# Summing seven half products of a weight tile in PSUM instead of on VectorE

## The chip, the cores and the metric

The kernel runs on one core of one Trainium2 chip. The metric is device time in microseconds (us): the median of several executions, and beside it one execution that the hardware profiler recorded. In the profile PE is TensorE (PEld its weight loads), DVE is VectorE, ACT is ScalarE, POOL is GpSimd and SP is SyncE.

## The reference

One block of a hybrid backbone over 512 latent tokens with a prefix of 256 context tokens, model width 1024, all in float32. The change lies in the first of the two matrix products of each feed-forward layer:

```python
def swiglu(u, wi, wo):
    gate, up = jnp.split(u @ wi, 2, axis=-1)      # wi: 1024 x 5632
    return (jax.nn.silu(gate) * up) @ wo          # wo: 2816 x 1024

def ffn_half(t, m, s, nw, wi, wo):
    u = modulate(t, nw, m[3 * s], m[3 * s + 1])
    return t + 0.5 * m[3 * s + 2] * swiglu(u, wi, wo)

# in the block: first layer over 512 latent + 256 context tokens,
h = ffn_half(h, lat_m, 0, ...); hc = ffn_half(hc, ctx_m, 0, ...)
# then the token mixer (linear attention and a recurrence), then the second layer over the 512 latent tokens
h = ffn_half(h, lat_m, 2, ...)
return rmsnorm(h, final_norm_w)
```

## The kernel before

Features lie on the partitions, tokens on the free axis. Every operand of a matrix product is split into a high part and a low part (`split`, L70: a cast on ScalarE, L75, then a subtraction on VectorE, L76), and a product is the sum of three matmuls: high by high, high by low, low by high.

A tile of `wi` is 1024 input features by 256 output features. Both of its dimensions and the tokens are cut in halves, and the four quadrants (128 features by half of the tokens) are made from seven half products instead of eight, of sums and differences of the halves. `half_items` (L173) makes the seven weight operands, four of them by sums on GpSimd (L180, tile `ws`). The token operands are the halves of the modulated tokens `u`, and four sums `T[0]` to `T[3]` (`half_sums`, L203), named by `half_operands` (L197) in the order of use. `half_gemm` (L224) does one tile: seven times 12 matmuls (L237) of N columns, N = 384 in the first layer and 256 in the second. In the kernel before each half product has a PSUM bank of its own, seven of the eight per tile. ScalarE copies the first to SBUF (L240, tile `hu`), and VectorE makes all sums out of it and the other banks: seven additions in a tile (L229).

`half_pair` (L757) calls `half_gemm` twice, for a gate tile and for the up tile of the same features. `gate` puts SiLU on each finished quadrant (ScalarE, L763, in SBUF). `up` multiplies each quadrant into it (VectorE, L769), and `keep` (L744) splits a finished row of 128 features (`ah` on ScalarE, `al` on VectorE) for the second product. There are 10 such pairs in each layer, 20 tiles of `wi`, so 40 tiles and 280 half products in all. The first pair of each layer goes another way (`start_both`, `first_latent`, evacuated by L753 and L754).

Weights go through a ring of split pieces (six in the first layer, eight in the second): when a half product is done, `done_w` (L136) frees its piece, and the piece six or eight places on is split into it. Between the pairs stand the second products with `wo` (`down`, L779, matmuls in L167), and in the first layer the work of the modulation is spread between the half products by `fill` (VectorE L448 and L450, matmuls L473 and L510).

A scheduler orders the instructions of each engine when the kernel is built, by the order of the program and its own estimate of when operands are ready. On the chip each engine takes its list strictly in that order.

Of the kernel before, what the change touches and what calls it, by code (L numbers as in the profile page):

```python
# [17 lines left out]
P = 128  # L18
# [16 lines left out]
class Block:  # L35
    """The block with features on the partitions and tokens on the free axis."""
# [12 lines left out]
    # ---------------------------------------------------------------- helpers  # L49
# [4 lines left out]
    def psum(self, pairs):  # L54
        """PSUM as so many pairs of banks, and single banks."""
        self.banks.close()
        self.pairs = pairs
        pool = lambda n: self.banks.enter_context(self.tc.tile_pool(name=self.n("ps"), bufs=n, space=PSUM, reuse_waits="tile"))
        if pairs:
            self.ps = pool(pairs)  # L60
        self.pss = pool(8 - 2 * pairs)

    def big(self):
        """[128, 1024] in PSUM."""
        return self.ps.tile([P, 1024], F32, tag="mm", name=self.n("mm"))
# [12 lines left out]
    def load_raw(self, parts, kts):  # L78
        """parts: (dram matrix, first row, first column, columns)."""
# [13 lines left out]
    def ring(self):  # L93
        """Room for 512 columns of a split operand: hi, lo."""
# [4 lines left out]
    def load_w(self, parts, kts=KT):  # L99
        """Split weights as a list of pieces of two row tiles: hi, lo."""  # L100
# [9 lines left out]
    def stream(self, items):  # L110
        """Operands in the order of their use: (pieces of the ring, function that makes them)."""
# [5 lines left out]
    def grow(self, pool, slots, raws):  # L117
        """More room for the ring, used after the one that it has."""
# [21 lines left out]
    def piece_items(self, part):  # L140
        """A tile of weights as items of one piece each."""
# [15 lines left out]
    def gemm(self, jobs, segs, kts=KT, order=None):  # L157
        """jobs: (psum or list of banks, weights, first column, columns); segs: (first psum column, columns, x(kt) -> hi, lo)."""
# [13 lines left out]
    # ------------------------------------------------- products of halves  # L172
    def half_items(self, w, r0, c0):  # L173
        """Operands of the seven products of a [1024, 256] tile of weights cut in halves both ways, in their order."""
# [8 lines left out]
        def make(i):  # L183
            if i == 0:
                st["raw"] = self.load_raw([(w, r0, c0, 256)], KT)
                s3 = sub(a(0, 0), a(0, 1))
                s1 = sub(a(0, 1), a(1, 1), ALU.add)
                s2 = sub(s1, a(0, 0))
                st["w"] = [a(0, 0), a(1, 0), s3, sub(a(1, 0), s2), s2, a(1, 1), s1]
# [7 lines left out]
    def half_operands(self, u):  # L197
        """Token operands of the seven products: u(k, t, kt) -> hi, lo of half k of the features and half t of the tokens."""
        o = lambda k, t: lambda kt: u(k, t, kt)
        v = lambda j: lambda kt: self.T[j][kt]  # L200
        self.hx = [o(0, 0), o(1, 0), v(2), o(1, 1), v(1), v(3), v(0)]

    def half_sums(self, kt, x0, x1, last=None):  # L203
        """Sums of the halves of row tiles kt and kt + 4: x0 whole values of the first tokens, x1 of the others with the bias still to add;
        returns the first and the last sum, still whole."""
# [18 lines left out]
    def half_gemm(self, N, out, fill):  # L224
        """The products of one tile of weights: out(i, j) is where quadrant i, j (features, tokens) goes, out(i, j, c) follows it."""
        nc = self.nc
        banks = []
        t = self.tmp.tile([P, N], F32, tag="hu", name=self.n("hu"), bufs=2)
        add = lambda o, x, y: nc.vector.tensor_tensor(out=o, in0=x, in1=y, op=ALU.add)  # L229
        for i in range(7):  # L230
            h, l = self.next_w()
            ps = self.small()[:, :N]
            banks.append(ps)
            for kt in range(4):
                xh, xl = self.hx[i](kt)
                for j in range(3):
                    nc.tensor.matmul(ps, (h, h, l)[j][:, kt, :], (xh, xl, xh)[j], start=kt == 0 and j == 0, stop=kt == 3 and j == 2)  # L237
            self.done_w()
            if i == 0:
                nc.scalar.copy(t, ps)  # L240
            elif i == 1:
                c = out(0, 0)
                add(c, t, ps)
                out(0, 0, c)
            elif i == 4:
                add(t, t, ps)
                c22, c12 = out(1, 1), out(0, 1)
                add(c22, t, banks[2])
                add(c12, t, banks[3])
            elif i == 5:  # L250
                c = out(1, 0)
                add(c, c22, ps)
                out(1, 0, c)
            elif i == 6:
                add(c12, c12, ps)
                out(0, 1, c12)
                add(c22, c22, ps)
                out(1, 1, c22)
            fill(i)

    def useg(self, s, t0=0, w=None):
        """Segment of the modulated tokens of stream s (0 latents, 1 context) for gemm."""
# [15 lines left out]
    # ---------------------------------------------------------------- setup  # L278
    def columns(self, g, parts):
        """Vectors of the inputs as columns over the partitions, 128 features each."""  # L280
# [47 lines left out]
    def setup_rest(self):  # L328
        """The vectors that the first feed-forward layer doesn't need."""
# [22 lines left out]
    def lru_scales(self):  # L352
        """-8 softplus(-lam) per channel, with exp by exact halving steps and a short series."""
# [39 lines left out]
    # ---------------------------------------------------------------- adaLN  # L393
    def ada_first(self, c, t, whole):
        """256 features of chunk c for both streams on TensorE, as rows: of the whole map or of its parts; returns what is left to trace."""
# [22 lines left out]
    def ada_turn(self, c, t, rows):  # L418
        """The rows as columns."""
# [21 lines left out]
    def ada_mul(self, raw, acc, ns, k):  # L441
        """Products and sums over two row tiles on VectorE."""
# [18 lines left out]
    def ada_gate(self):  # L461
        """Gate of the first sub-layer on TensorE, in pieces to trace between other work."""
# [27 lines left out]
    def gate_cols(self, t, rows):  # L490
        """The rows as columns."""
# [10 lines left out]
    def ada_sum(self, acc, ns, dst, r0):  # L502
        """Sums over the partitions on TensorE, exact in two parts, and the rows to dst."""
# [1167 lines left out]
```

## Time and profile before

| what | us |
|---|---|
| median of three runs | 1595.04 |
| lowest and highest of the three | 1594.09, 1595.93 |
| span of the profiled execution, first to last instruction | 1593.6 |
| PE busy in it | 1543.3 |
| DVE busy | 1258.2 |
| ACT busy | 782.0 |
| POOL busy | 332.6 |

The profiled execution has no time of its own beside its span, which lies 0.5 to 2.3 us under the three runs. A matmul counts as busy until its modelled end, and matmuls overlap, so PE can be busy throughout and still have started its matmuls late: the distance from one start to the next tells how fast it goes.

### The profile page before, as it was taken

What the parts mean: (1) busy time and instruction counts of PE and PEld (TensorE: products, weight loads), DVE (VectorE), ACT (ScalarE), POOL (GpSimd) and SP (SyncE); (2) the same over time, 40 slices, a digit from 0 to 9 for tenths busy, and PEclk for the clock granted to TensorE, in tenths of its full rate; (3) what the DMA queues carried; (4) which work ended last, traced back from release to release, by engine and by line L of the source; (5) the groups of instructions that cost most, each with busy time, mean ns of one, the idle gap of its engine ahead of it and who ended that gap; (6) DMA issues with size and microseconds to landing.
All of it is one profiled execution on the core that took longest, in us unless ns stands there. A gap on an engine that the chain in (4) does not pass through costs nothing.

```text
span 1593.6 us, 24995 instructions
## 1 busy us (share of the span) xinstructions
PE 1543.3 (97%) x9288; PEld 1383.8 (87%) x9288; DVE 1258.2 (79%) x2232; ACT 782.0 (49%) x1353; POOL 332.6 (21%) x265
## 2 busy tenths in 40 slices
PE   7979999999999999999999999999998899999998
PEld 4778898999998987899897888878898898999897
DVE  5997899999997688776577577777768996797694
ACT  6354233432342457455354487777444644354355
POOL 0441121311322124000000100000016451451322
PEclk9999999999999999999999999999999999999999
DMA  9214434341533233121216223224443224233233
GB/s 335 78 47 146 123 96 139 91 146 57 159 113 95 82 106 107 33 64 47 68 62 186 73 64 90 78 68 140 153 149 115 67 80 143 70 107 120 93 113 113
DMA packets 169238, 167.83 MB, mean 105 GB/s; under 512 B 7683, under 2 KB 166685, under 8 KB 169117
## 3 DMA queue, kind: packets, MB, share of 16 engines
q1 hardware_dynamic: 168092, 163.88, 33.8%
q0 software_dynamic: 1024, 2.36, 0.5%
q8 instruction: 73, 1.20, 0.3%
q14 instruction: 49, 0.39, 0.1%
HBM read 164.08 MB, written 2.10 MB: 104 GB/s over the span
## 4 chain that ended last, share of the span: by engine, by line
PE 71%; DVE 12%; ACT 5%; issue 3%; POOL 1%; DVEq 0%; ACTq 0%
PE sm L237 27%; PE sm L167 22%; PE mm L167 16%; DVE wl L76 3%; PE mm L1255 1%; PE sm L1055 1%; DVE th L1288 1%; PE mm L1082 1%; PE sm L1002 1%; ACT wh L75 1%; DVE rg L1286 1%; ACT e L1274 1%; ACT th L1273 1%; DVE xc L1238 1%; ACT rg L1275 1%
## 5 line engine op out<-in xcount | busy, mean ns | idle before, releaser
L76 DVE TENSOR_TENSOR wl<-raw,wh 128x512 fp32r<-128x512 f32 x420 | 312.6, 755 | 96.4 <-ACT wh L75 93.9
L75 ACT CAST wh<-raw 128x512 fp32r<-128x512 f32 x420 | 254.7, 618 | 255.5 <-PE sm L167 107.0
L167 PE MATMUL sm<-ah,wh 128*128 128x512 f32 (+1 forms) x576 | 172.5, 341 | 0.0
L167 PE MATMUL sm<-al,wh 128*128 128x512 f32 (+1 forms) x576 | 172.5, 340 | 0.0
L167 PE MATMUL sm<-ah,wl 128*128 128x512 f32 (+1 forms) x576 | 172.2, 339 | 0.0
L75 ACT CAST wh<-ws 128x512 fp32r<-128x512 f32 x160 | 97.5, 618 | 127.3 <-PE sm L167 66.4
L167 PE MATMUL mm<-ul_lo,wh 128*128 128x512 f32 x352 | 141.6, 402 | 0.0
L167 PE MATMUL mm<-ul_hi,wh 128*128 128x512 f32 x352 | 140.9, 400 | 0.0
L167 PE MATMUL mm<-ul_hi,wl 128*128 128x512 f32 x352 | 139.8, 397 | 0.0
L76 DVE TENSOR_TENSOR wl<-ws,wh 128x512 fp32r<-128x512 f32 x160 | 128.5, 814 | 12.4 <-ACT wh L75 12.0
L450 DVE SCALAR_TENSOR_TENSOR acc<-apiece,cs,acc 128x256 f32<-128x256 f32 x224 | 121.3, 564 | 15.1 <-DMA apiece<-in_w_ada_dram 12.8
L180 POOL TENSOR_TENSOR ws<-raw 128x512 f32<-128x512 f32 x40 | 60.1, 1503 | 331.7 <-DMA raw<-in_ffn_wi_dram 155.8
L237 PE MATMUL sm<-u_hi,wh 128*128 128x384 f32 x320 | 108.8, 340 | 6.1 <-ACT s L753 6.1
L167 PEld LDWEIGHTS sm<-al,wh 128*128 128x128 f32 x576 | 98.4, 189 | 12.9 <-issue 0.2
L167 PEld LDWEIGHTS sm<-ah,wh 128*128 128x128 f32 x576 | 98.5, 188 | 12.8 <-ACT ah L75 0.3
L167 PEld LDWEIGHTS sm<-ah,wl 128*128 128x128 f32 x576 | 98.4, 188 | 12.6
L237 PE MATMUL sm<-u_hi,wl 128*128 128x384 f32 x320 | 108.4, 339 | 0.0
L237 PE MATMUL sm<-u_lo,wh 128*128 128x384 f32 x320 | 108.4, 339 | 0.0
L797 DVE SCALAR_TENSOR_TENSOR h_l<-sm,hg,h_l 128x512 f32<-128x512 f32 (+1 forms) x80 | 55.1, 693 | 46.5 <-PE sm L167 46.5
L1220 POOL DMA_DIRECT2D gwr<-in_lru_wr_dram x8 | 5.8, 730 | 376.2 <-PE mm L167 255.7
L606 POOL TENSOR_TENSOR ssq<-ssq,t 128x256 f32<-128x256 f32 (+1 forms) x30 | 28.0, 934 | 263.7 <-ACT t L604 263.5
L167 PEld LDWEIGHTS mm<-ul_hi,wh 128*128 128x128 f32 x352 | 66.2, 188 | 15.8 <-issue 0.5
(496 smaller groups left out, 4346.4 us busy)
## 6 DMA issues: line engine op xcount, KB each, us to landing
raw<-in_ffn_wi_dram SPq DMA_DIRECT2D x88, 512.0 KB
apiece<-in_w_ada_dram SPq DMA_DIRECT2D x112, 256.0 KB
raw<-in_ffn_wo_dram SPq DMA_DIRECT2D x48, 512.0 KB
raw<-in_w_in_dram SPq DMA_DIRECT2D x48, 512.0 KB
araw<-in_w_ada_dram SPq DMA_DIRECT2D x8, 1024.0 KB
raw<-in_w_o_dram SPq DMA_DIRECT2D x16, 512.0 KB
raw<-in_w_in_dram SPq DMA_DIRECT2D x16, 256.0 KB
raw<-in_w_out_gla_dram SPq DMA_DIRECT2D x8, 512.0 KB
```

Source lines behind the costliest of these rows:

```text
L75: nc.scalar.copy(hi, src)
L76: (nc.gpsimd if eng == "p" else nc.vector).tensor_tensor(out=lo, in0=src, in1=hi.bitcast(F32), op=ALU.subtract)
L167: nc.tensor.matmul(dst[:cols, d0 : d0 + width], wk, xs, start=(kt == 0 and i == 0), stop=(kt == kts - 1 and i == 2),)
L180: nc.gpsimd.tensor_tensor(out=t, in0=x, in1=y, op=op)
L237: nc.tensor.matmul(ps, (h, h, l)[j][:, kt, :], (xh, xl, xh)[j], start=kt == 0 and j == 0, stop=kt == 3 and j == 2)
L450: nc.vector.scalar_tensor_tensor(out=acc[:, s, :], in0=raw[:, kt, :], scalar=c, in1=acc[:, s, :], op0=ALU.mult, op1=ALU.add)
L606: (nc.vector if kt == KT - 1 or s else nc.gpsimd).tensor_tensor(out=acc, in0=acc, in1=dst, op=ALU.add)
L797: nc.vector.scalar_tensor_tensor(out=h, in0=o[s][:, t0 : t0 + w], scalar=self.hg[:, s, m : m + 1], in1=h, op0=ALU.mult, op1=ALU.add)
L1002: nc.tensor.matmul(ps[:, :DV], (xh, xl, xh)[i][:, kt, t0 : t0 + P], w[kt // 2][i // 2][:, kt % 2, :], start=kt == 0 and i == 0, stop=kt == ...
L1055: nc.tensor.matmul(ps[:, :DV], kt_[d][:, n, :], v[:, p, :], start=True, stop=True)
L1082: nc.tensor.matmul(dst, states[d][p][:, es], dec[d][0][:, t], start=False, stop=d == 1)
L1238: nc.vector.scalar_tensor_tensor(out=dst, in0=x[:, :, a0 + o : L - a1 + o], scalar=w(j), in1=dst, op0=ALU.mult, op1=ALU.add)
```

## The change

The seven half products of a tile are taken in another order and accumulate in four banks, in the order a, c, a, b, a, d, a. TensorE thus adds four of the seven into bank a. Quadrant (1,0) is what bank a holds after the seventh. The three earlier contents of bank a (after the first, third and fifth product) are copied by ScalarE to SBUF, in place of one copy before. VectorE adds these copies to the other banks: one addition for quadrants (0,0) and (1,1), two for (0,1), none for (1,0), whose SiLU or multiplication reads PSUM directly. The order of the token operands, of the weight operands and of three sums on GpSimd changes with it. `keep` now follows quadrants (0,1) and (1,0). The text of the diff also drops comments, left out here.

```diff
 def half_items ... make(i):
-                s3 = sub(a(0, 0), a(0, 1))
                 s1 = sub(a(0, 1), a(1, 1), ALU.add)
                 s2 = sub(s1, a(0, 0))
-                st["w"] = [a(0, 0), a(1, 0), s3, sub(a(1, 0), s2), s2, a(1, 1), s1]
+                s3 = sub(a(0, 0), a(0, 1))
+                st["w"] = [a(0, 0), a(1, 0), s2, s1, s3, sub(a(1, 0), s2), a(1, 1)]
...
 def half_operands(self, u):
-        self.hx = [o(0, 0), o(1, 0), v(2), o(1, 1), v(1), v(3), v(0)]
+        self.hx = [o(0, 0), o(1, 0), v(1), v(0), v(2), o(1, 1), v(3)]
...
 def half_gemm(self, N, out, fill):
-        banks = []
-        t = self.tmp.tile([P, N], F32, tag="hu", name=self.n("hu"), bufs=2)
-        add = lambda o, x, y: nc.vector.tensor_tensor(out=o, in0=x, in1=y, op=ALU.add)
-        for i in range(7):
+        copies = []
+
+        def copy(ps):
+            t = self.tmp.tile([P, N], F32, tag="hu", name=self.n("hu"), bufs=5)
+            nc.scalar.copy(t, ps)
+            copies.append(t)
+
+        bank = {}
+        for i, b in enumerate("acabada"):
             h, l = self.next_w()
-            ps = self.small()[:, :N]
-            banks.append(ps)
+            first = b not in bank
+            if first:
+                bank[b] = self.small()[:, :N]
+            ps = bank[b]
             for kt in range(4):
                 xh, xl = self.hx[i](kt)
                 for j in range(3):
-                    nc.tensor.matmul(ps, (h, h, l)[j][:, kt, :], (xh, xl, xh)[j], start=kt == 0 and j == 0, stop=kt == 3 and j == 2)
+                    nc.tensor.matmul(ps, (h, h, l)[j][:, kt, :], (xh, xl, xh)[j], start=first and kt == 0 and j == 0,
+                                     stop=kt == 3 and j == 2, skip_group_check=not first)
+            if i in (0, 2, 4):
+                copy(ps)
             self.done_w()
-            if i == 0:
-                nc.scalar.copy(t, ps)
-            elif i == 1:
-                c = out(0, 0)
-                add(c, t, ps)
-                out(0, 0, c)
+            if i == 1:
+                out(0, 0, copies[0], ps)
             elif i == 4:
-                add(t, t, ps)
-                c22, c12 = out(1, 1), out(0, 1)
-                add(c22, t, banks[2])
-                add(c12, t, banks[3])
+                out(1, 1, copies[2], bank["b"])
             elif i == 5:
-                c = out(1, 0)
-                add(c, c22, ps)
-                out(1, 0, c)
+                out(0, 1, copies[1], ps, bank["b"])
             elif i == 6:
-                add(c12, c12, ps)
-                out(0, 1, c12)
-                add(c22, c22, ps)
-                out(1, 1, c22)
+                out(1, 0, ps)
             fill(i)
...
 def half_pair(m):
-            def gate(i, j, c=None):
-                if c is not None:
-                    self.last_silu = nc.scalar.activation(c, c, AF.Silu)
-                return at(i, j)
-
-            def up(i, j, c=None):
-                if c is None:
-                    return self.tmp.tile([P, N], F32, tag="c", name=self.n("c"), bufs=3)
-                nc.vector.tensor_tensor(out=at(i, j), in0=at(i, j), in1=c, op=ALU.mult)
-                if j == 1:
+            add = lambda o, x, y: nc.vector.tensor_tensor(out=o, in0=x, in1=y, op=ALU.add)
+
+            def gate(i, j, x, y=None, z=None):
+                o = at(i, j)
+                if y is not None:
+                    add(o, x, y)
+                    if z is not None:
+                        add(o, o, z)
+                    x = o
+                self.last_silu = nc.scalar.activation(o, x, AF.Silu)
+
+            def up(i, j, x, y=None, z=None):
+                for t in (y, z):
+                    if t is not None:
+                        add(x, x, t)
+                nc.vector.tensor_tensor(out=at(i, j), in0=at(i, j), in1=x, op=ALU.mult)
+                if (i, j) in ((0, 1), (1, 0)):
                     keep(ss[i])
```

## Rows read from the trace of the kernel before

**Rows 1.** The page: busy time by engine, and slices of the span.

```profile
PE 1543.3 (97%) x9288; PEld 1383.8 (87%) x9288; DVE 1258.2 (79%) x2232; ACT 782.0 (49%) x1353; POOL 332.6 (21%) x265
...
DVE  5997899999997688776577577777768996797694
```

**Rows 2.** Waits of PE, whole span: total us, times, longest us.

```profile
PE sm L237 <- ACT s L753: 6.1, 2, 4.4
PE sm L237 <- DVE hu L229: 4.1, 4, 2.0
...
PE sm L473 <- DVE al L76: 2.1, 1, 2.1
PE sm L473 <- ACT ah L75: 1.8, 1, 1.8
```

**Rows 3.** Busy us by stage: PE, PEld, DVE, ACT, POOL, granted clock, DMA share, GB/s.

```profile
281.00:341.00 60.00, 60.00 (x352) 59.48 (x349) 58.32 (x105) 25.73 (x47) 14.54 (x10) 1.00 0.37 111
...
1246.00:1319.00 73.00, 66.17 (x516) 64.66 (x515) 72.04 (x108) 35.26 (x75) 37.18 (x27) 0.95 0.29 86
...
1269.20:1272.50 3.30, 3.30 (x18) 3.30 (x17) 3.30 (x8) 1.39 (x4) 0.94 (x1) 0.50 0.54 165
1372.00:1453.00 81.00, 81.00 (x678) 80.81 (x677) 77.58 (x133) 42.84 (x85) 36.53 (x23) 1.00 0.34 105
```

**Rows 4.** Timeline of DVE, two additions merged in a row, each layer.

```profile
296.81 1.00 DVE L229 TENSOR_TENSOR c<-hu,sm 128x384 f32<-128x384 f32 x2
...
1269.49 0.74 DVE L229 TENSOR_TENSOR s<-hu,sm 128x256 f32<-128x256 f32 x2
```

**Rows 5.** Groups of ACT by line: the copy of each layer (busy, mean ns).

```profile
L240 ACT COPY hu<-sm 128x384 f32<-128x384 f32 x17 | 8.0, 471 | 0.0
...
L240 ACT COPY hu<-sm 128x256 f32<-128x256 f32 x13 | 4.8, 367 | 0.0
```

**Rows 6.** Timeline of PE: starts of half products two and three of a tile.

```profile
297.87 0.34 PE L237 MATMUL sm<-u_hi,wh 128*128 128x384 f32 x1
...
299.95 0.34 PE L237 MATMUL sm<-T20h,wh 128*128 128x384 f32 x1
```

**Rows 7.** Timeline of ACT beside the tile of Rows 6.

```profile
302.35 0.83 ACT L75 CAST ah<-s 128x768 fp32r<-128x768 f32 x1 [5.91 <-DVE s L769]
303.09 0.62 ACT L75 CAST wh<-ws 128x512 fp32r<-128x512 f32 x1
```

**Rows 8.** Timeline of DVE up to that cast.

```profile
295.74 0.54 DVE L229 TENSOR_TENSOR hu<-hu,sm 128x384 f32<-128x384 f32 x1
...
298.81 0.54 DVE L769 TENSOR_TENSOR s<-s,c 128x384 f32<-128x384 f32 x1
299.27 1.51 DVE L450 SCALAR_TENSOR_TENSOR acc<-apiece,cs,acc 128x256 f32<-128x256 f32 x1
300.70 0.54 DVE L229 TENSOR_TENSOR c<-c,sm 128x384 f32<-128x384 f32 x1
...
301.77 0.55 DVE L769 TENSOR_TENSOR s<-s,c 128x384 f32<-128x384 f32 x1
```

**Rows 9.** Timeline of PE and of ACT in the first tile of all.

```profile
96.24 0.52 PE L237 MATMUL sm<-T20h,wh 128*128 128x384 f32 x1
...
99.09 0.62 ACT L75 CAST wh<-ws 128x512 fp32r<-128x512 f32 x1
```

**Rows 10.** Timeline of PE and ACT, start of the second layer.

```profile
1281.34 0.28 PE L237 MATMUL sm<-T10h,wh 128*128 128x256 f32 x1
1281.46 0.28 PE L237 MATMUL sm<-T10l,wh 128*128 128x256 f32 x1
...
1309.54 0.28 PE L237 MATMUL sm<-T20h,wh 128*128 128x256 f32 x1
...
1286.65 0.62 ACT L75 CAST wh<-ws 128x512 fp32r<-128x512 f32 x1
...
1316.15 0.60 ACT L75 CAST wh<-raw 128x512 fp32r<-128x512 f32 x1
```

## The prediction

> **What bounds the kernel now.** I read the page first: PE is busy 97% of the span, DVE 79%, but DVE's slices stand at 7 to 9 tenths in the feed-forward layers, at both ends of the span [rows 1]. Then busy time by stage. In the first layer, from 281 to 341 us, PE is busy all 60 us and DVE 58.3 of them; in the second, from 1372 to 1453, PE all 81 and DVE 77.6; only where the second layer begins, from 1246 to 1319, does PE fall behind (66.2 of 73) with DVE full (72.0) [rows 3]. Last the waits of PE. Matmul L237 waits 6.1 us for the evacuation before the first tile (L753), 4.1 us in four waits for an addition that still reads a bank (L229), and the filler's matmuls L473 wait 3.9 us for ACT and DVE [rows 2]. All of them lie at the beginnings of the two layers. So in the steady tiles PE sets the time, and DVE, nearly as busy, is late without PE noticing: bank and weights are ready long before PE needs them. Less work for DVE pays nothing there by itself. The question is whether PE stays free of DVE's lateness.
>
> **What is removed.** Three additions of seven per tile. A pair of them takes 1.00 us in the first layer and 0.74 in the second [rows 4], so one about 0.5 and 0.37, and a tile is relieved of 1.5 and 1.1 us of DVE: 20 x 1.5 + 20 x 1.1 = 52 us. By stage: four tiles in the 60 us leave DVE 52.3 there, eight tiles in the 81 leave 68.8, six in the 73 leave 65.4 [rows 3]. Three banks per tile come free; what that can give is the four waits for L229, 4.1 us [rows 2].
>
> **What is added on ACT.** Two copies per tile, 0.47 and 0.37 us [rows 5], 34 us in all. ACT is busy 25.7 of the 60 us and 42.8 of the 81 [rows 3]; with 3.8 and 5.9 more it stays near half. As work they cost nothing, as long as ACT isn't waiting when they come.
>
> **What stays.** The number of matmuls. Adding into a bank that holds a sum is what the later matmuls of each product do now, so I take no other rate. The sums on GpSimd are the same four in another order, their results used earlier or later by a product or two, with six or eight pieces of lead: nothing, and a few us for one late piece at most. No transfer is moved.
>
> **The new wait.** Half products three, five and seven write the bank that ACT has to have copied after one, three and five. One other product stands between: 2.08 us in the first layer [rows 6], 12 x 0.12 = 1.44 in the second [rows 10]. A copy and handing over, for which I add 0.1 us (an estimate: ACT starts 0.03 us after the multiplication that it waited for has ended [rows 7, 8], and there are two such steps), need 0.57 and 0.47. So the copy is hidden if ACT reaches it within about 1.3 or 0.8 us of the product's end, since that end lies 0.2 us behind the next start. ACT takes its list in order; when a cast (`ah`) or SiLU ahead of the copy waits for DVE, the copy waits too, and behind it now PE.
>
> Where ACT would be can be read from the old trace: the cast `wh` of the piece that a half product frees is ready at the same moment as the new copy, which stands directly ahead of it. In most of the 120 places this cast starts at once. Where not, the third product's start would be late by the cast's start, plus copy and handing over, less the old start:
> first tile of all: 99.09 + 0.57 - 96.24 = 3.4 us [rows 9];
> a steady tile of the first layer: 303.09 + 0.57 - 299.95 = 3.7, where ACT had waited 5.9 us for DVE's last multiplication [rows 6, 7];
> start of the second layer: 1286.65 + 0.47 - 1281.34 = 5.8, and the largest of all, 1316.15 + 0.47 - 1309.54 = 7.1 [rows 10].
> The lateness of one stretch of tiles between two down projections is one and the same queue: PE pays its largest value once. Read so, the ten stretches have 4.7, 0, 3.9, 3.7, 1.1, 2.7, 0 in the first layer and 7.1, 4.6, 1.3 in the second, 29 us together. This is the price if DVE's relief didn't reach the copies; with full relief it is nothing.
>
> **The relief, place by place.**
> *Start of the first layer.* The copy is 3.4 us late, but a tile later PE waits 3.9 us for the filler's split anyway [rows 2], so the new wait takes the place of the old one. I take -0.5. Ends: the wait stays beside the new one, +3.4; no copy late and the old wait gone, -3.9.
> *Steady tiles of the first layer.* In the tile of rows 7 the copy waits for the multiplication of quadrant (0,1), at 301.77. It now belongs to half product six instead of seven, with two additions and one weight split fewer ahead of it, 2 x 0.5 + 0.6; if it also passes the filler's L450 (1.51), 3.1 [rows 8]. I take 2.0, near the sure part: 1.7 of the 3.7 stays, 0.7 of the 2.7 in the same way. At the 3.9, two tiles before it give 3.0 more, and nothing stays; nor of the 1.1. Together +2.4, between 0 and 11.4.
> *Start of the second layer.* Two tiles lie before the 5.8: 5.8 - 2 x 1.1 = 3.6. Before the 7.1 lie five: 1.6, less than already paid. Of the waits for banks, 2.0 us lie ahead of that place and are in its times, and the other 2.1 behind it fall away: +1.5. Ends: -4.1 and +7.1.
> *Later tiles of the second layer.* The lateness grows by some 1.9 us per pair up to 4.6, and a pair is relieved of 2.2: nothing, at most 5.9.
> A long wait of PE costs more than itself: behind the one of 2.0 us the granted clock is 0.50, the lower level, from 1269.2 to 1272.5 [rows 3], and 3.3 us at half speed lose 1.65. One such stretch may come in the steady tiles and one may go at a start; I count none and keep 1.65 each way.
>
> Sum: -0.5 + 2.4 + 1.5 + 0 = +3.4 us. The profiled execution spans 1593.6, which gives 1597.0; the median of the runs lies 1.4 above that span, so 1598.4.
>
> **The rivals.**
> *The copies hold PE (slower).* The scheduler's list was made from its own estimate, and ACT stands behind DVE where that is too short; a list made for fewer additions can be as far off. Then the 29 us of lateness are paid less what falls away at the starts, 4.1 and 3.9: up to +21, with half of the relief +12, so 1607 to 1616. For it: ACT waits of 5.9 us [rows 7]. Against it: DVE has 8 us in 60 to spare after the change. It decides where ACT comes to a copy over 1.3 us after its product. The Trainium skill (PSUM — Partial Sum Buffer, Summary: rules for kernel authors) speaks for this rival: whoever reads PSUM while a matmul runs should target a different bank, and guard by bank. The traces so far show no half product that waits for such a reader inside its tile, since each had its own bank.
> *The starts gain (faster).* From 1246 to 1319 DVE is full; 6.6 us less work could pass to PE directly, and the waits for banks (4.1) and for the filler (3.9) would go with up to two stretches at half clock (3.3). All of it is -11; with half, some -6: 1589. It needs the copies on time at the starts, where DVE is most behind, so the relief would have to cover 3.4 and 5.8 us that I see covered by 1.5 to 2.2. The Trainium skill (Perfetto Trace Analysis, Optimization Strategy) speaks for it: the same gap again and again on the engine that should be full can mean too little PSUM. Here there are four such gaps, 4.1 us in 1594.
> *Nothing measurable.* DVE isn't on the path for most of the span, and the small terms cancel: 1593 to 1598. It is the lower part of my forecast.
>
> **Chances and range.** The forecast, +3.4 with its own range of -1 to +9 us, has 0.55; the copies 0.23; the starts 0.22. About 0.2% (3.2 us) is what a measurement of this kernel can tell from no change. The forecast lies on that line: 0.35 of it I give to no change, 0.20 to slower. So faster 0.22, same 0.35, slower 0.43. For 8 in 10 the range reaches into both rivals: 1588 to 1612.
>
> **What would show it.** Right: DVE's busy time falls to about 1206 us and ACT's rises to about 816; waits of L237 for L229 are gone; in their place stand waits of L237 for the new copy, the longest in the first pair after a down projection and at the start of the second layer, a handful, under 10 us together; most copies start within 0.2 us of their product. Wrong: waits for the copy in most tiles and the clock at half in steady stretches (the slower rival); no such waits over 1 us and both starts shorter (the faster one); another distance than 0.17 or 0.12 us between matmuls that add to a full bank.

## The result and the profile after

The changed kernel takes 1634.97 us (median of 4 runs, 1634.0 to 1637.5) against 1595.25 for the kernel before, run beside it (4 runs): a ratio of 1.0251, interval 1.0238 to 1.0264. It is 39.7 us slower, outside the range of 1588 to 1612. The profiled execution spans 1632.2 us, 38.6 more than that of before: over the span PE is idle 30.2 us longer and busy 8.4 us longer.

In the kernel after, the half products' matmul stands on L245, the copy on L232, the additions on L760, the SiLU on L769, the multiplication on L775. The page first, the lines that answer to [rows 1]:

```profile
PE 1551.7 (95%) x9288; PEld 1390.4 (85%) x9288; DVE 1237.2 (76%) x2112; ACT 812.9 (50%) x1433; POOL 338.6 (21%) x265
...
DVE  5996998978976688676577587769668984795684
```

DVE has 120 instructions fewer, as meant, but is only 21.0 us less busy (1258.2 to 1237.2), not 52. Then PE's waits, which answer to [rows 2]:

```profile
PE sm L245 <- ACT hu L232: 37.0, 20, 5.7
...
PE sm L245 <- ACT s L752: 6.2, 2, 4.4
```

The waits for an addition that still reads a bank (4.1 us) are gone; in their place PE waits 37.0 us in 20 places for the new copy, in 19 of them before the third half product of a tile. Busy time by stage, in stretches that hold about as many matmuls as those of [rows 3], and two short stretches behind a wait (columns as there):

```profile
285.00:349.00 64.00, 60.47 (x350) 59.20 (x348) 55.77 (x96) 30.24 (x57) 12.52 (x10) 1.00 0.35 108
1265.00:1343.00 78.00, 66.32 (x514) 65.29 (x514) 72.27 (x102) 42.47 (x92) 39.89 (x27) 0.93 0.27 86
1396.00:1487.00 91.00, 84.20 (x681) 82.88 (x680) 81.10 (x115) 49.97 (x105) 38.89 (x24) 0.98 0.34 103
...
1458.50:1461.90 3.40, 3.40 (x18) 3.40 (x18) 3.40 (x3) 1.13 (x4) 3.32 (x3) 0.50 0.40 131
...
1301.40:1304.70 3.30, 3.30 (x18) 3.30 (x17) 3.30 (x5) 1.71 (x4) 2.92 (x2) 0.51 0.50 153
```

The eight tiles in which PE was busy all of 81 us now take 91, and PE is idle for 6.8 of them. It is also busy 3.2 us longer with about as many matmuls. A part of that is clock: behind one of the waits below (1457.27) the granted clock is at 0.50, the lower level, for 3.4 us, which at half speed lose 1.7; the stage stood at 1.00 before. Where the rest of the 3.2 goes wasn't followed. The loss is in the steady tiles, not only where a layer begins.

A smaller part lies between the two layers, where PE now waits for DVE once (this wait isn't in the trace of before; why it comes wasn't followed):

```profile
PE sm L1008 <- DVE x L1134: 2.5, 1, 2.5
```

These are the third half products of six tiles of the second layer, PE's timeline (start, duration, in brackets the wait and what ended it):

```profile
1411.51 0.39 PE L245 MATMUL sm<-T10h,wh 128*128 128x256 f32 x1 [1.89 <-ACT hu L232]
...
1422.24 0.38 PE L245 MATMUL sm<-T10h,wh 128*128 128x256 f32 x1 [0.49 <-ACT hu L232]
...
1433.92 0.39 PE L245 MATMUL sm<-T10h,wh 128*128 128x256 f32 x1 [1.47 <-ACT hu L232]
...
1445.31 0.39 PE L245 MATMUL sm<-T10h,wh 128*128 128x256 f32 x1 [1.18 <-ACT hu L232]
...
1457.27 0.39 PE L245 MATMUL sm<-T10h,wh 128*128 128x256 f32 x1 [1.77 <-ACT hu L232]
...
1545.00 0.39 PE L245 MATMUL sm<-T10h,wh 128*128 128x256 f32 x1 [1.89 <-ACT hu L232]
```

Five tiles in a row pay, each anew. Why, is seen by following the last of these waits backwards through three engines. ACT:

```profile
1543.54 1.14 ACT L75 CAST ah<-s 128x512 fp32r<-128x512 f32 x2 [2.76 <-DVE s L775]
1544.58 0.36 ACT L232 COPY hu<-sm 128x256 f32<-128x256 f32 x1
1544.84 0.62 ACT L75 CAST wh<-raw 128x512 fp32r<-128x512 f32 x1
```

DVE:

```profile
1535.72 5.19 DVE L76 TENSOR_TENSOR wl<-ws,wh 128x512 fp32r<-128x512 f32 x3
1540.83 0.74 DVE L760 TENSOR_TENSOR hu<-hu,sm 128x256 f32<-128x256 f32 x2
1541.49 0.41 DVE L775 TENSOR_TENSOR s<-s,hu 128x256 f32<-128x256 f32 x1
1541.82 0.68 DVE L76 TENSOR_TENSOR wl<-raw,wh 128x512 fp32r<-128x512 f32 x1
1542.42 0.41 DVE L760 TENSOR_TENSOR hu<-hu,sm 128x256 f32<-128x256 f32 x1
1542.76 0.41 DVE L775 TENSOR_TENSOR s<-s,sm 128x256 f32<-128x256 f32 x1
1543.09 0.41 DVE L775 TENSOR_TENSOR s<-s,hu 128x256 f32<-128x256 f32 x1
```

POOL:

```profile
1535.32 1.62 POOL L180 TENSOR_TENSOR ws<-ws,raw 128x512 f32<-128x512 f32 x1
1536.91 1.74 POOL L180 TENSOR_TENSOR ws<-raw 128x512 f32<-128x512 f32 x1
1538.61 1.75 POOL L180 TENSOR_TENSOR ws<-raw,ws 128x512 f32<-128x512 f32 x1
```

The copy at 1544.58 stands in ACT's list behind both casts `ah` of the tile before. They wait 2.76 us for DVE's last multiplication, at 1543.09. DVE comes to its additions only at 1540.83, because three splits of weights take 5.19 us, 1.73 each; and exactly there POOL makes three sums. A split alone takes 0.68 (the one at 1541.82). Over the whole span this group is what DVE's relief went into, 29.5 us more; the first fence is of before, the second of after (columns: busy, mean ns; idle before and what ended it):

```profile
L76 DVE TENSOR_TENSOR wl<-ws,wh 128x512 fp32r<-128x512 f32 x160 | 128.5, 814 | 12.4 <-ACT wh L75 12.0
```

```profile
L76 DVE TENSOR_TENSOR wl<-ws,wh 128x512 fp32r<-128x512 f32 x160 | 158.0, 1002 | 34.4 <-ACT wh L75 34.0
```

### The profile page after: what moved, and what is told of

Same layout as the page of the kernel before. It is cut to its first block, busy times and chain, and to the rows that moved or that the text cites. A ratio compares the mean times of both kernels' runs of the same rounds, so it can differ in the third digit from the quotient of the medians.

```text
span 1632.2 us, 24776 instructions
## 1 busy us (share of the span) xinstructions
PE 1551.7 (95%) x9288; PEld 1390.4 (85%) x9288; DVE 1237.2 (76%) x2112; ACT 812.9 (50%) x1433; POOL 338.6 (21%) x265
## 4 chain that ended last, share of the span: by engine, by line
PE 63%; DVE 13%; ACT 6%; issue 3%; POOL 1%; DMA 0%; DVEq 0%; ACTq 0%
PE sm L245 21%; PE sm L167 19%; PE mm L167 16%; DVE wl L76 3%; PE mm L1261 1%; PE sm L1061 1%; DVE th L1294 1%; ACT wh L75 1%; PE mm L1088 1%; PE sm L1008 1%; DVE s L775 1%; DVE rg L1292 1%; ACT e L1280 1%; ACT th L1279 1%; DVE xc L1244 1%
## 5 line engine op out<-in xcount | busy, mean ns | idle before, releaser
L76 DVE TENSOR_TENSOR wl<-raw,wh 128x512 fp32r<-128x512 f32 x420 | 308.8, 744 | 130.8 <-ACT wh L75 128.3
L76 DVE TENSOR_TENSOR wl<-ws,wh 128x512 fp32r<-128x512 f32 x160 | 158.0, 1002 | 34.4 <-ACT wh L75 34.0
L180 POOL TENSOR_TENSOR ws<-raw,raw 128x512 f32<-128x512 f32 x40 | 55.9, 1399 | 499.6 <-DMA raw<-in_ffn_wi_dram 331.2
L245 PE MATMUL sm<-u_hi,wh 128*128 128x384 f32 x320 | 109.5, 342 | 6.2 <-ACT s L752 6.2
L245 PE MATMUL sm<-u_lo,wh 128*128 128x384 f32 x320 | 108.9, 340 | 0.0
L245 PE MATMUL sm<-u_hi,wl 128*128 128x384 f32 x320 | 108.8, 340 | 0.0
```

Source lines behind the costliest of these rows:

```text
L76: (nc.gpsimd if eng == "p" else nc.vector).tensor_tensor(out=lo, in0=src, in1=hi.bitcast(F32), op=ALU.subtract)
L180: nc.gpsimd.tensor_tensor(out=t, in0=x, in1=y, op=op)
```

## Experiments

Two theories stood at first. A: the new wait itself, because ACT comes to the first copy of a tile behind casts and SiLUs that wait for DVE. B: what the change did to GpSimd's sums (another order, in a burst), which slows DVE; then the copies are only the place where it shows. All times are medians with the ratio to the kernel before, run beside them, and its interval.

### The wait alone, and ACT's order

**e4_before_with_wait**, the kernel before with nothing but the wait:

```diff
-            ps = self.small()[:, :N]
+            ps = banks[0] if i == 2 else self.small()[:, :N]
...
-            self.done_w()
             if i == 0:
                 nc.scalar.copy(t, ps)
-            elif i == 1:
+            self.done_w()
+            if i == 1:
```

> The kernel before with the new wait alone: the third half product is written into the bank of the first, once ScalarE has copied that; still seven additions on VectorE. Theory A: this wait is most of the loss; read off the trace of the kernel before it costs 20 to 29 us, 1615 to 1625, or more if each tile pays again. Theory B: the wait alone costs under 10 us, 1605 at most, since the sums stand in their old order.

1623.43 us, ratio 1.0172 (1.0156 to 1.0187). Its waits of PE:

```profile
PE sm L237 <- ACT hu L239: 31.2, 18, 8.2
```

With all seven additions, without any adding into a full bank, and with GpSimd's sums in their old order, one wait per tile costs 27 us. The coupling is real and was there to be had in the kernel before.

**e1_casts_behind_copy**, the kernel after; the splits of both finished rows of an up tile (casts on ACT, and the subtractions on DVE that need them) and, where no second product is due, the last two SiLUs of a gate tile are held back until the next tile's first copy (`run_late` issues them behind it; `keep` with True holds its split back):

```diff
             if i in (0, 2, 4):
-                copy(ps)
+                ins = copy(ps)
+                if i == 0:
+                    self.run_late(ins)
...
-                self.last_silu = nc.scalar.activation(o, x, AF.Silu)
+                if (i, j) in ((0, 1), (1, 0)) and not held:
+                    self.late.append(silu_)
+                else:
+                    silu_()
...
-                    keep(ss[i])
+                    keep(ss[i], True)
```

> The changed kernel; only the order on ScalarE differs: the casts of a finished up tile and the last two SiLUs of a gate tile are put behind the first copy of the tile that follows. Theory A (the 37 us in which TensorE waits for the copy come from ScalarE's list, where these casts and SiLUs stand ahead of the copy and wait for VectorE): the waits for the copy fall from 37 us to under 8, the time to 1598 to 1606 us. Theory B (VectorE itself is late, since the sums on GpSimd now come in a burst and slow its weight splits): the wait moves to the other copies or to the weights, the time stays over 1620.

1611.83 us, ratio 1.0101 (1.0084 to 1.0118); 20.8 us of waits for copies in 17 places, between what the two theories gave. This order carries 23 of the 39.7 us. What is left has the same form one step later, e1's ACT and then its DVE (copy L233, SiLU L787, addition L777, split L77):

```profile
1423.50 0.42 ACT L787 ACTIVATE s<-s 128x256 f32<-128x256 f32 x1 [2.25 <-DVE s L777]
1423.83 1.12 ACT L76 CAST wh<-raw 128x512 fp32r<-128x512 f32 x2
1424.86 0.37 ACT L233 COPY hu<-sm 128x256 f32<-128x256 f32 x1
```

```profile
1418.29 4.85 DVE L77 TENSOR_TENSOR wl<-ws,wh 128x512 fp32r<-128x512 f32 x3
1423.06 0.74 DVE L777 TENSOR_TENSOR s<-hu,sm 128x256 f32<-128x256 f32 x2
```

Now a copy later in the tile stands behind a SiLU that waits for an addition behind three slow splits.

**e6_own_bank**, the wait for the first copy taken away:

```diff
-        for i, b in enumerate("acabada"):
+        for i, b in enumerate("acebede"):
```

> The kernel after, but the third half product opens a bank of its own (five banks a tile), so that no product writes the bank of the first copy; copies, additions, sums and their places stay. The first product is thereby left out of three quadrants. If the wait for the first copy behind casts and SiLUs is the loss, the 35 us before the third product go, with some 5 us of half clock: 1594 to 1600, and waits for copies under 4 us. If it is VectorE's lateness, wherever it meets TensorE, the fifth product waits in place of the third: 1612 to 1630.

1626.73 us, ratio 1.0196 (1.0181 to 1.0211). Theory A as it stood falls here:

```profile
PE sm L245 <- ACT hu L232: 31.1, 18, 4.6
```

No half product can wait for the first copy any more, and PE waits nearly as long, now before the fifth product. ACT's list stays late over the next two products, and PE meets it at the next bank.

**e10_copy_on_vector**, the three copies on DVE:

```diff
-            nc.scalar.copy(t, ps)
+            nc.vector.tensor_copy(t, ps)
```

> The kernel after with its three copies on VectorE instead of ScalarE; all else stays. VectorE gets some 50 us more. If the cause is ScalarE's list (casts and SiLUs ahead of the copy), the copy no longer stands behind them: waits of TensorE under 15 us and 1600 to 1612. If VectorE itself is late at the end of every tile, the copy waits there as it did: waits of 30 us or more and 1630 to 1660.

1641.17 us, ratio 1.0290 (1.0275 to 1.0306).

```profile
PE sm L245 <- DVE hu L232: 34.2, 29, 5.5
```

Off ACT's list, the copies hold PE nearly as long (DVE has 35 us more to do here). So DVE itself is late; ACT's list, by e1, decides how much of that lateness reaches the copies.

### What the relief is worth, and distance

**e8_before_four_adds**, the kernel before, less three additions:

```diff
-                add(t, t, ps)
...
-                add(c12, c12, ps)
...
-                add(c22, c22, ps)
```

> The kernel before with three of its seven additions per tile left out (the fifth product reaches no quadrant and the seventh none); banks, copies, sums and products stay. It prices the relief alone. VectorE's busy time falls by about 52 us. If VectorE holds TensorE only at the two beginnings, 1586 to 1595: the whole relief is worth at most 10 us. If it is worth more than 15 us, VectorE was a bound where the prediction saw none.

1591.03 us, ratio 0.9976 (0.9965 to 0.9986): the relief alone is worth 4 us. DVE was busy 1232.7 us, 25.5 less than before instead of 52; the splits of sums rose to 879 ns.

**e7_three_between**, operands and sums in the order of before, four additions, four banks:

```diff
-        for i, b in enumerate("acabada"):
+        for i, b in enumerate("acbdaba"):
...
-            if i in (0, 2, 4):
+            if i in (0, 2, 3, 4):
                 copy(ps)
...
-            elif i == 4:
-                out(1, 1, copies[2], bank["b"])
             elif i == 5:
-                out(0, 1, copies[1], ps, bank["b"])
+                out(1, 0, copies[3], ps)
             elif i == 6:
-                out(1, 0, ps)
+                out(0, 1, copies[2], ps)
+                out(1, 1, copies[1], ps)
```

> The whole computation with the same four additions, also in four banks, but in the order of products and sums of the kernel before: product five adds to the bank of product one (three others stand between), product six to that of product three (two between), product seven to that of product five (one between); four copies on ScalarE instead of three. If the distance between a tile's first copy and the next use of its bank is what matters, the waits nearly go: 1590 to 1600, TensorE's waits for copies under 8 us. If any adding into copied banks ties TensorE to VectorE, or ScalarE's added copies make it late, 1612 to 1640.

1605.93 us, ratio 1.0067 (1.0050 to 1.0084); waits for copies 17.0 us in 15 places, longest 2.6. Distance helps, but not fully: e7 is 29 us faster than the kernel after, and 24 faster than e2 below, which has the old order of GpSimd's sums as e7 does. Of the 15 waits, seven (7.2 us) lie before product seven, whose bank has one product between, as in the kernel after; four (4.4) before product six, and three (2.8) before product five.

**e9_one_sum**, the kernel before with one sum on PE and three products between:

```diff
-            ps = self.small()[:, :N]
+            ps = banks[0] if i == 4 else self.small()[:, :N]
...
-            if i == 0:
+            if i in (0, 4):
+                t = self.tmp.tile([P, N], F32, tag="hu", name=self.n("hu"), bufs=2)
                 nc.scalar.copy(t, ps)
...
-                add(t, t, ps)
```

(The matmuls of product five all have start=False.)

> The kernel before, whole, with one of its sums moved to TensorE: the fifth product adds to the bank of the first (three products stand between, 8.3 and 5.8 us), ScalarE copies that bank after the first and the fifth product, VectorE makes six additions, and no product writes a bank after the second copy. If the loss hangs on the distance between a copy and the next use of its bank against a lateness of ScalarE of 2 to 6 us, nothing waits here: 1592 to 1597, TensorE's waits for copies under 2 us. If any use of a copied bank costs, 1600 to 1612.

1601.0 us, ratio 1.0038 (1.0025 to 1.0050); waits for copies 7.2 us in 6 places, longest 3.7. A miss by some 4 us, into the lower end of the other range: the longest of these waits, at the start of the second layer, shows a lateness beyond even three products, and the other five, of 0.46 to 0.85 us, lie in later tiles or in the first layer.

### The order of GpSimd's sums

**e2_sums_as_before** (kernel after) and **e3_before_sums_moved** (kernel before) move one line in opposite directions; **e5_behind_sums** is e1 and e2 at once.

```diff
+                s3 = sub(a(0, 0), a(0, 1))
                 s1 = sub(a(0, 1), a(1, 1), ALU.add)
                 s2 = sub(s1, a(0, 0))
-                s3 = sub(a(0, 0), a(0, 1))
```

> The changed kernel with one line moved: the difference of the first two quarters on GpSimd is made first again, as in the kernel before. Theory A: under 5 us of change, 1630 to 1637. Theory B: the weight splits out of the sums fall from 1002 ns back to about 815, VectorE loses 20 us of busy time or more, and the time falls by 10 to 25 us.

> The kernel before with that line alone moved the other way (sum, difference of it, then the difference of the first two quarters). Theory A: no change, 1593 to 1598, whatever happens to the splits, since TensorE doesn't wait for VectorE there. Theory B: the splits out of the sums rise from 815 ns towards 1000; if VectorE's lateness counts by itself the time rises by over 5 us.

> The two changes of the earlier runs at once on the kernel after: the last casts and SiLUs of a tile behind the next tile's first copy, and GpSimd's third sum first again as before. The computation is whole. Alone the first took 1635 to 1612, the second to 1629. If the two causes are separate (late casts ahead of the copy, and a burst of sums that slows VectorE's weight splits), the gains add: 1612 - 5.5 = 1606, with TensorE's waits for the copy at 15 to 18 us instead of 20.8. If the order of the sums matters only because the splits delay those same casts, nothing is left for it: 1611 to 1614 and waits near 20.

e2: 1629.49 us, ratio 1.0207 (1.0181 to 1.0234). e3: 1604.18, ratio 1.0044 (1.0029 to 1.0059). e5: 1607.00, ratio 1.0075 (1.0060 to 1.0090), waits for copies 15.9 us. The order is worth some 5 to 8 us either way, and the two gains add as far as the intervals tell. It explains only a part of the slower splits: they take 966 ns on average in e2 (1002 in the kernel after) and 847 in e3 (814 before). It isn't the main part of the loss. So theory B in its narrow form, the order, falls too.

### The sums themselves

In e6 and e10 DVE's lateness met PE wherever it could, and in e8 DVE got less relief than it had instructions fewer, with slower splits. So theory C: any sum on POOL beside a split slows the split, and that is the lateness. **e11_no_sums** (after) and **e12_before_no_sums** (before):

```diff
-            t = self.sp.tile([P, 4, P], F32, tag="ws", name=self.n("ws"), bufs=self.sums)
-            nc.gpsimd.tensor_tensor(out=t, in0=x, in1=y, op=op)
-            return t
+            return x
```

> The kernel after with the four sums of weights per tile on GpSimd left out: four half products take a quarter of the raw weights instead. VectorE's splits then have no GpSimd work beside them. If slowed splits (1.6 us instead of 0.7) are what makes VectorE and behind it ScalarE late at the copies, TensorE's waits for copies fall from 37 to under 10 us and the time to 1590 to 1602. If the order of ScalarE's list is enough, waits stay over 20 us: 1615 to 1630. To be compared with the same cut of the kernel before.

> The kernel before with the same cut: no sums of weights on GpSimd. It is the measure for the other run. By either theory TensorE sets the time in the steady tiles, so only the beginnings of the two layers gain: 1585 to 1594.

e11: 1582.94 us, ratio 0.9924 (0.9909 to 0.9938). e12: 1575.85, ratio 0.9882 (0.9867 to 0.9897). Both are faster than expected: in the kernel before, too, the sums cost 19 us. Without sums the change costs 7.1 us instead of 39.7, and its waits for copies are two, both where a layer begins (the wait of 2.5 us between the layers stays):

```profile
PE sm L243 <- ACT hu L230: 9.2, 2, 5.3
```

And DVE's relief arrives: 1169.9 us busy in e12, 1124.8 in e11, 45 less. This cut takes away two things, the work beside DVE and the wait for a sum that is ready late. **e15_sums_unread** (after) and **e16_before_sums_unread** (before) keep the first alone:

```diff
             nc.gpsimd.tensor_tensor(out=t, in0=x, in1=y, op=op)
-            return t
+            return x
```

> The kernel after with GpSimd making its four sums per tile as always, but nothing reads them: the splits take raw weights, as in the run without sums (1583). It parts the two ways in which a sum can hurt. If it is the work beside VectorE, the loss comes back: 1610 to 1635, with waits for copies over 20 us. If it is that splits and casts wait for a late sum, it stays gone: 1580 to 1595.

> The same cut of the kernel before, as the measure: sums made on GpSimd and read by nothing. Without sums it took 1576, with them 1595. If the work beside VectorE is the whole of their price, 1590 to 1597; if their readiness is, 1574 to 1580.

e15: 1636.34 us, ratio 1.0263 (1.0247 to 1.0279). e16: 1596.87, ratio 1.0018 (1.0007 to 1.0028). The whole loss is back, 39.5 us between the two, with sums that nothing reads:

```profile
PE sm L245 <- ACT hu L232: 39.9, 21, 6.8
```

**e13_sums_on_vector** (after) and **e14_before_sums_on_vector** (before) keep the sums and take the work beside DVE away:

```diff
-            nc.gpsimd.tensor_tensor(out=t, in0=x, in1=y, op=op)
+            nc.vector.tensor_tensor(out=t, in0=x, in1=y, op=op)
```

> The kernel after, whole, with the four sums of weights per tile on VectorE instead of GpSimd: 160 more instructions there, about 0.6 us each by the other additions, some 100 us, but nothing beside them on GpSimd. If what hurts is that a split takes 1.6 us beside a GpSimd sum, VectorE's total stays near 1225 and its lumps shrink: waits for copies 10 to 25 us, 1600 to 1622. If VectorE's load is what hurts, it is as late as ever or more: 1630 to 1650.

> The kernel before, whole, with the four sums per tile on VectorE. Without the sums VectorE was busy 1170 us; 160 x 0.6 more make 1266, as now (1258). If the slowed splits are only VectorE time, nothing changes: 1590 to 1600. If the lumps hold TensorE at the beginnings of the layers, it gains: 1580 to 1590.

e13: 1595.51 us, ratio 1.0004 (0.9994 to 1.0013). e14: 1583.45, ratio 0.9925 (0.9911 to 0.9940). With 160 instructions more, DVE is busy less than in the kernel after, 1212.1 us. The same place as above, e13's DVE:

```profile
1499.33 0.69 DVE L76 TENSOR_TENSOR wl<-ws,wh 128x512 fp32r<-128x512 f32 x1
1499.93 0.69 DVE L180 TENSOR_TENSOR ws<-raw 128x512 f32<-128x512 f32 x1
1500.53 0.68 DVE L76 TENSOR_TENSOR wl<-ws,wh 128x512 fp32r<-128x512 f32 x1
1501.13 0.69 DVE L180 TENSOR_TENSOR ws<-raw,ws 128x512 f32<-128x512 f32 x1
1501.73 0.69 DVE L76 TENSOR_TENSOR wl<-ws,wh 128x512 fp32r<-128x512 f32 x1
1502.34 0.74 DVE L760 TENSOR_TENSOR hu<-hu,sm 128x256 f32<-128x256 f32 x2
```

and its ACT:

```profile
1505.05 1.14 ACT L75 CAST ah<-s 128x512 fp32r<-128x512 f32 x2 [0.75 <-DVE s L775]
1506.09 0.36 ACT L232 COPY hu<-sm 128x256 f32<-128x256 f32 x1
```

Sum and split take 0.69 each, one after the other, where on two engines each took 1.7 at once. ACT's list has the same order, both casts ahead of the copy, but they wait 0.75 us instead of 2.76, and no wait of PE is left there (product three starts at 1506.51). The waits for copies are down to these:

```profile
PE sm L245 <- ACT hu L232: 9.4, 4, 8.0
```

What is left of the change's price, 12.1 us against e14, lies in good part where the second layer begins, with the wait of 8.0: in the same stretch PE does 49 matmuls fewer in e13 (first fence) than in e14 (second).

```profile
1225.00:1310.00 85.00, 75.67 (x607) 74.59 (x606) 75.69 (x152) 51.14 (x110) 11.95 (x8) 0.93 0.26 80
```

```profile
1225.00:1310.00 85.00, 81.90 (x656) 80.13 (x655) 81.33 (x169) 49.81 (x106) 11.96 (x8) 0.98 0.27 81
```

Another 2.5 us are the wait between the layers, which e13 has and e14 hasn't. From 77 to 140 us, where the first layer begins, both do as many matmuls (300 and 299).

One thing isn't parted: in e13 the splits are short, and DVE is also busy 25 us less in all. But e2, whose DVE is busy 1226.6 us, 14.5 more than in e13, pays 33.9 us of waits for copies, so the total alone hardly makes the difference.

### Both remedies

**e17_three_between_vector** is e7 and e13's edit, **e18_behind_vector** e1 and e13's edit.

> Both remedies, whole: four additions with three half products between a tile's first copy and the next use of its bank (alone 1606), and the four sums of weights on VectorE (alone with the change 1595.5, with the kernel before 1583.5). If the change is worth its three additions once its copies meet no late ScalarE, it beats the 1583.5: 1576 to 1582, waits for copies under 3 us. If even short splits leave the copies late, 1584 to 1594.

> The kernel after, whole, with the last casts and SiLUs of a tile behind the next tile's first copy (alone 1612) and the four sums on VectorE (alone 1595.5). If both remedies work on the same lateness, it comes to 1582 to 1592 with waits for copies of 3 to 8 us; if the places in ScalarE's list no longer matter once the splits are short, it stays at 1594 to 1598.

e17: 1582.48 us, ratio 0.9925 (0.9911 to 0.9940). e18: 1591.53, ratio 0.9977 (0.9968 to 0.9987), waits for copies 8.9 us, of which one is 8.0. e17 is as fast as e14, not faster. Its time lies just above the lower of the two ranges, and two waits for copies are left, 5.7 us, one where each layer begins; so what the three additions per tile are worth when nothing waits for the copies isn't shown. In e18 the waits are hardly fewer than in e13 (9.4 us); the one of 8.0 stays. e14 and e17, which compute the full result, beat the two kernels; e14 does it with a single word changed.

## Why the prediction was wrong

The kernel went the way of the rival "The copies hold PE", and beyond it (1607 to 1616). ACT's 812.9 us against the forecast of 816, the end of the waits for additions, and a distance of 0.12 us between matmuls that add to a full bank (in the fifth product of a tile they start at 1535.81, 1535.93, 1536.05) came out as said. These steps failed:

**"The relief, place by place"** failed, and it is the largest part of the miss. The sum let DVE's relief take away most of the copies' lateness; the copies wait as if hardly any had come (us; the last column holds PE's waits for copies in the kernel after):

| place | counted | its end without relief | waits, places |
|---|---|---|---|
| first layer, start | -0.5 | +3.4 | 3.7, 1 |
| first layer, steady tiles | +2.4 | +11.4 | 10.6, 6 |
| second layer, start | +1.5 | +7.1 | 11.7, 5 |
| second layer, later tiles | 0 | +5.9 | 11.0, 8 |

Only the first came out as said: its wait replaces the filler's 3.9. The price without relief, 29 us, was about right as a sum: e4, which has no relief, pays 31.2. The relief failed to reach the copies for two reasons, the next two points.

**The sums on GpSimd, "nothing, a few us at most"**, failed. Their order is worth 5 to 8 us (e2, e3). Their running beside DVE is worth 32.6 of the 39.7: the change costs 39.7 us with them, 7.1 without, 39.5 with sums that nothing reads. The 52 us were right as a count of instructions and wrong as time: 21.0 arrived, because the splits of sums went from 814 to 1002 ns. Without sums 45 arrive. That relief pays little where PE sets the time was right: 4 us in e8.

**Where ACT would be** failed in part. At the place shown the copy does stand directly ahead of the weight cast of the freed piece (1544.58, 1544.84). But in the old list one cast `ah` stood ahead of this place and the other behind, as here in the second layer, in the trace of before:

```profile
1428.72 0.62 ACT L75 CAST ah<-s 128x512 fp32r<-128x512 f32 x1 [4.17 <-DVE s L769]
1429.25 0.37 ACT L240 COPY hu<-sm 128x256 f32<-128x256 f32 x1
...
1431.70 0.62 ACT L75 CAST ah<-s 128x512 fp32r<-128x512 f32 x1 [1.56 <-DVE s L769]
```

The list made for the new kernel puts both ahead of the copy, and the second needs the last multiplication of the tile before; moving them back, with the SiLUs of the other tiles, brought 23 us (e1). Yet the order alone isn't the cause: e13 has the same at the place shown, and beside its wait of 8.0 us at a beginning the other three waits for copies are 1.4 us together.

**"PE pays its largest value once"** failed as a mechanism: in the later tiles of the second layer two stretches were to pay 5.9 us at most, and eight waits of 0.49 to 1.89 paid 11.0, five tiles in a row. The lateness isn't one queue that drains; it is made anew. Where the splits are short (e13), these tiles have one wait of 0.27.

**The clock**, counted as none with 1.65 us either way, cost more. The mean granted clock is 0.984 in the kernel after and 0.989 before; over 1632.2 and 1593.6 us that is an estimated 8.6 us of full speed lost on top, about the 8.4 that PE is busy longer. The stretches at 0.50 and 0.51 in the windows begin behind waits of 1.77 us (1457.27) and 2.09 (1300.92).

**The start of the second layer** was sized too low even where the other cause is gone: +1.5, with an end of +7.1, and e13 pays a wait of 8.0 there.

## What to carry to other kernels

Before work is put where the fullest engine waits for a copy, ask what stands ahead of that copy in its engine's list and whom that waits for; a chain through two engines that was late and hidden becomes late and paid, tile after tile. Price an engine's relief from a trace in which its instructions run alone: here a split took 0.69 us alone and 1.73 beside GpSimd, so more than half of what the three additions saved was spent again, while moving GpSimd's work onto the "full" VectorE made the kernel 12 us faster. When two remedies each take away much of a loss, look for what both depend on, and test that by keeping the work and dropping its result.

## What the runs showed of the hardware

**A GpSimd sum and a VectorE split at once.** Both read two tensors in SBUF. In the run with the sums on DVE the 160 splits of sums take 687 ns on average; in the kernel after, with the sums on POOL, they take 1002 on average, and three in a row beside three sums 1.73 us each (1535.72). The Trainium skill (SBUF — State Buffer, SBUF: two separate sides) has the rule: a VectorE instruction with two inputs in SBUF and a GpSimd instruction that reads SBUF contend for one pair of ports, and whichever comes first holds it for its whole length. The trace agrees that they hold each other up. That each is held for the other's whole length isn't shown: the shortest of these sums takes 1.26 us in the kernel after and a split alone 0.69, 1.95 together, while a pair takes 1.73 there (times on POOL are rough).

**An addition that reads PSUM isn't slowed.** The additions of `hu` and a bank take 479 ns on average in the kernel after and 482 without sums; the multiplication of two tensors in SBUF takes 561 and 488:

```profile
L760 DVE TENSOR_TENSOR hu<-hu,sm 128x384 f32<-128x384 f32 (+1 forms) x80 | 37.5, 479 | 3.6 <-PE sm L245 3.3
L775 DVE TENSOR_TENSOR s<-s,hu 128x384 f32<-128x384 f32 (+1 forms) x60 | 33.6, 561 | 0.8
```

```profile
L758 DVE TENSOR_TENSOR hu<-hu,sm 128x384 f32<-128x384 f32 (+1 forms) x80 | 37.8, 482 | 7.5 <-PE sm L243 7.4
...
L773 DVE TENSOR_TENSOR s<-s,hu 128x384 f32<-128x384 f32 (+1 forms) x60 | 29.3, 488 | 0.9
```

So the change took away the three additions per tile that GpSimd doesn't disturb and left VectorE with the instructions that it does.
